# Batching three groups of VectorE instructions in a two-layer decoder trunk with an expert mixer

## The chip, the cores and the metric

One core of a Trainium2 chip runs the whole program. Its engines are TensorE (PE in the rows), which multiplies matrices, VectorE (DVE), ScalarE (ACT), GpSimd (POOL, which here only issues gathers) and SyncE (SP, which issues the other transfers). Each engine works through its own instructions in order and waits on semaphores for the others. The metric is the device time of one execution in microseconds (us), lower is better.

## The reference

The input is 512 tokens of width 1024. Each of two layers has a token mixer (retention and a gated recurrence), a cross-attention into 256 memory tokens, and a channel mixer that retrieves experts. The change is in the channel mixer:

```
s1 = q1 . sub_k1   s2 = q2 . sub_k2        # 8 heads, 128 keys each half
v1, i1 = top_k(s1, 16);  v2, i2 = top_k(s2, 16)
cand = v1[:, None] + v2[None, :]           # keep the best 16 of the pair sums
vals, ci = top_k(cand, 16)
idx = i1[ci // 16] * 128 + i2[ci % 16];    gates = softmax(vals)
act = gelu(peer_u[idx] . x)                # 16384 experts of width 1024
out = sum over 8 * 16 experts of gates * act * peer_v[idx]
```

## The kernel before

The channel mixer (`peer`) handles 384 of the 512 tokens densely: it multiplies all 128 blocks of 128 experts with all 384 tokens and weights the result by a gate table that is zero where an expert was not chosen. The last tile of 128 tokens is done by gathering expert rows, on POOL and DVE.

- **Keys.** For each of 16 half heads PE makes scores for the four token tiles, and DVE takes the best 16 with five instructions (`top16`, lines 834 to 839). One instruction for each half head and tile (line 853) turns the 16 indices into scaled key numbers. There are 64 of these in a layer.
- **U stage.** A loop over 128 blocks j of `peer_u`: 24 matmuls of 384 columns each on PE (three products for each of eight chunks, lines 216 to 218), then a gelu on ACT (`ag`, line 1030). Between the blocks the loop advances three generators at rates set by hand: `route` (line 878), `scatter` (line 979) and `rows_u` (line 776).
- **route(t)**, in the order of tiles 3, 0, 1, 2: the sums of the candidates, their best 16, and then for each head a look-up of the expert's number: a difference of 16 by 50 candidates (line 905) and a minimum of its absolute value (line 907), then the gates, and for tiles 0 to 2 three transposes on PE.
- **scatter**, for tiles 0 to 2 as each has been routed: for each group of four tokens DVE makes one-hot rows (`oab`, line 947, two buffers), ACT scales them by the gates (`ob`, line 953, two buffers; four instructions, or eight where the gate is in two halves), PE multiplies the two (`sm`, line 963 or 971) and ACT, in half of the groups with DVE, puts the result into `stage`. Every 16 tokens SP writes one stage of 1 MB to DRAM (`gates<-stage`, line 977).
- **rows_u**, after route(3): for each of 128 places a gather of one expert row for each of the 128 gathered tokens (`rows`, three buffers) and one product with the token's row on DVE (line 782).
- **V stage.** The loop over blocks runs from the last group of eight to the first. At the head of a group the gates of the group are read back from DRAM (`big<-gates` for the first one, `gg` later; line 807). For each block DVE multiplies activations by gates (`wv`, line 1066), `split` makes the two halves `ws` (ACT line 222, DVE line 223), and PE adds 24 matmuls of 384 columns into eight accumulators (`out`). `rows_v` advances beside it and adds one gathered row to `yrow` on DVE (line 800).
- **Weights.** For every block SP loads 512 KB (`w`, four buffers), ACT makes `wh` (line 200) and DVE makes `wl` (line 202), three buffers each; PE needs both.

Code is written in this order, but a list scheduler places the instructions of each engine by modelled times before the program is built, so the order on an engine may differ from that of the source, and a change of a few instructions can move many others.

Of the kernel before, what the change touches and what calls it, by code (L numbers as in the profile page):

```python
# [19 lines left out]
D = 1024  # L20
# [6 lines left out]
PH = 8  # L27
# [126 lines left out]
def trunk(ctx: ExitStack, tc: tile.TileContext, A, out, dbg=None):  # L154
# [84 lines left out]
    def C(n, t=cst, base=NTAB):  # L239
        o, w = CST[n]  # L240
        return t[:, o - base:o - base + w]
# [519 lines left out]
    def peer(l):  # L761
# [14 lines left out]
        def rows_u():  # L776
            for k in range(PH * K):
                r = gp.tile([128, D], F32, name="rows", bufs=3)
                nc.gpsimd.indirect_dma_start(out=r, out_offset=None, in_=A["peer_ur"].rearrange("l e d -> (l e) d"),  # L779
                                             in_offset=bass.IndirectOffsetOnAxis(ap=irow[:, 0, k:k + 1], axis=0))  # L780
                s = gp.tile([128, D], F32, name="prod", bufs=1)
                nc.vector.scalar_tensor_tensor(s, r, 1.0, hrow, op0=OP.mult, op1=OP.mult, accum_out=arow[:, k:k + 1])
                yield 1.3
                if k % 32 == 31:
                    ks = slice(k - 31, k + 1)
                    nc.scalar.activation(wrow[:, ks], arow[:, ks], AF.Gelu_apprx_tanh)
                    nc.vector.tensor_mul(wrow[:, ks], wrow[:, ks], grow[:, ks])
# [22 lines left out]
        with tpool(name=f"pr{l}", bufs=1) as rt, tpool(name=f"ph{l}", bufs=1) as hp, tpool(name=f"pps{l}", bufs=4, space=PS) as psum, \  # L810
# [30 lines left out]
            with tpool(name=f"pk{l}", bufs=1) as kp:  # L841
                def keys(hd, i, q, sk):
                    sc = psm.tile([128, TT, NK], F32, name="sm")
                    for t in range(TT):
                        nc.tensor.matmul(sc[:, t], lhsT=q[:, t * 128:(t + 1) * 128], rhs=sk, start=True, stop=True)
                    yield
                    s = kp.tile([128, TT, NK], F32, name="sc", bufs=3)
                    nc.scalar.copy(s, sc)
                    for t in range(TT):
                        wk = kp.tile([128, NK], F32, name="wk", bufs=2)  # L850
                        idx = kp.tile([128, K], U32, name="idx", bufs=2)
                        top16(val[i][t][:, hd], idx, s[:, t], wk)
                        nc.vector.scalar_tensor_tensor(idf[i][t][:, hd], idx, (NK if i == 0 else 1.0) / IDS,
                                                       C("first") if i == 0 else C("iota")[:, 0:K],
                                                       op0=OP.mult, op1=OP.add)

                for c in range(2 * PH):
                    hd, i = divmod(c, 2)
# [12 lines left out]
                        token_rows()  # L871
                drain()

            pp = es.enter_context(tpool(name=f"pu{l}", bufs=1))
            pe = pp.tile([128, TD, 2], F32, name="pe")
            pg = pp.tile([128, 3, TD], F32, name="pg")

            def route(t):

                big = gp.tile([128, NTB * GRP * TB], F32, name="big")  # L880
                cand, cid = (big[:, o:o + PH * NC_].rearrange("p (h c) -> p h c", h=PH) for o in (0, PH * NC_))
                ohs = [big[:, o:o + K * NC_].rearrange("p (k c) -> p k c", k=K)
                       for o in (2 * PH * NC_, 2 * PH * NC_ + K * NC_)]
                for dst, a1, a2 in ((cand, val[0][t], val[1][t]), (cid, idf[0][t], idf[1][t])):
                    off = 0
                    for a in range(8):
# [13 lines left out]
                cf = rt.tile([128, PH, K], F32, name="cf", bufs=2)  # L900
                nc.vector.tensor_copy(cf, ci)
                ee = rt.tile([128, PH, K], F32, name="ee", bufs=2)
                for hd in range(PH):
                    oh = ohs[hd % 2]
                    nc.vector.tensor_sub(oh, cid[:, hd, None, :].to_broadcast([128, K, NC_]),
                                         cf[:, hd, :, None].to_broadcast([128, K, NC_]))
                    nc.vector.tensor_reduce(ee[:, hd], oh, axis=AX.X, op=OP.min, apply_absolute_value=True)
                    yield 1.8
                ei = rt.tile([128, 3, PH * K], I32, name="ei", bufs=1)
                nc.vector.tensor_scalar(ei[:, 2], ee.rearrange("p h k -> p (h k)"), IDS, None, op0=OP.mult)  # L910
                nc.vector.tensor_scalar(ei[:, 1], ei[:, 2], NK - 1, None, op0=OP.bitwise_and)
# [133 lines left out]
        with tpool(name=f"pv{l}", bufs=1) as vp, tpool(name=f"vps{l}", bufs=1, space=PS) as psum:  # L1045
# [10 lines left out]
            for j in v_order():  # L1056
                g, i = divmod(j, GRP)
                if i == 0:
                    gg = gates.get(g) or gate_group(vp, f"gg{g % 2}", g)
                    if j < NK - GC * GRP:  # L1060
                        ar = vp.tile([128, GRP, TD], F32, name=f"ar{(g + 1) % 2}")
                        nc.sync.dma_start(ar, acts[g])
                kept = j - (NK - GC * GRP)
                act = ar[:, i] if kept < 0 else last[kept // 4][:, i % 4]
                wv = vp.tile([128, TD], F32, name="wv", bufs=2)
                nc.vector.tensor_mul(wv.rearrange("p (b t) -> p b t", b=NTB),
                                     act.rearrange("p (b t) -> p b t", b=NTB), gg[:, :, i, :])
                ws = vp.tile([128, 2, TD], F32R, name="ws", bufs=max(3, NCM))
                split(ws, wv)
                pend.append((weights("v", l, j, ahead=1 if j == GRP - 1 else 2), ws))  # L1070
                if not GRP - NCM <= j < GRP:
                    products(j, pend.pop())
                credit += VPACE
                while credit > 0:
                    credit -= next(todo, VPACE)
# [92 lines left out]
```

## Time and profile before

| | |
|---|---|
| median of three runs | 3853.55 us (3851.89 to 3855.34) |
| the profiled execution, its span | 3855.28 us, 3853.2 us |
| PE busy | 3801.3 us, 99% of the span |
| DVE busy | 2999.6 us, 78% |
| ACT busy | 1900.1 us, 49% |
| POOL busy | 734.3 us, 19% |
| DMA | 877.06 MB, mean 228 GB/s |

In time, one layer is the mixer and the attention (about 0 to 668 us in the first layer), keys and the U stage (about 694 to 1379 us) and the V stage (about 1381 to 1921 us); the second layer repeats it about 1917 us later. A row of the timeline gives the start, the duration, the engine and line, what is written from what, how many instructions are merged (x), and in brackets how long the engine was idle before and what ended it. Instructions of DVE and ACT overlap by a little, so the distance from one start to the next is shorter than a duration.

### The profile page before, as it was taken

What the parts mean: (1) busy time and instruction counts of PE and PEld (TensorE: products, weight loads), DVE (VectorE), ACT (ScalarE), POOL (GpSimd) and SP (SyncE); (2) the same over time, 40 slices, a digit from 0 to 9 for tenths busy, and PEclk for the clock granted to TensorE, in tenths of its full rate; (3) what the DMA queues carried; (4) which work ended last, traced back from release to release, by engine and by line L of the source; (5) the groups of instructions that cost most, each with busy time, mean ns of one, the idle gap of its engine ahead of it and who ended that gap; (6) DMA issues with size and microseconds to landing.
All of it is one profiled execution on the core that took longest, in us unless ns stands there. A gap on an engine that the chain in (4) does not pass through costs nothing.

```text
span 3853.2 us, 56299 instructions
## 1 busy us (share of the span) xinstructions
PE 3801.3 (99%) x20636; PEld 3535.2 (92%) x20636; DVE 2999.6 (78%) x5556; ACT 1900.1 (49%) x3531; POOL 734.3 (19%) x517
## 2 busy tenths in 40 slices
PE   8999999999999999999999999999999999999998
PEld 7888888899999999999978888878999999999998
DVE  7449665999989968777854596659999898687877
ACT  5336444336778843333343363543367788333333
POOL 0000000013233323333200000000232333233432
PEclk9999999999999999999999999999999999999999
DMA  4222342268999989999722223322689999899995
GB/s 150 82 87 95 104 134 69 83 208 317 309 319 348 335 325 338 345 346 346 269 82 77 93 94 104 131 67 88 232 308 312 319 350 315 332 348 342 345 346 213
DMA packets 313476, 877.06 MB, mean 228 GB/s; under 512 B 24945, under 2 KB 131569, under 8 KB 305265
## 3 DMA queue, kind: packets, MB, share of 16 engines
q1 hardware_dynamic: 239472, 605.01, 44.3%
q0 software_dynamic: 73728, 268.47, 19.8%
q8 instruction: 162, 2.65, 0.3%
q14 instruction: 114, 0.93, 0.1%
HBM read 776.13 MB, written 97.26 MB: 227 GB/s over the span
## 4 chain that ended last, share of the span: by engine, by line
PE 88%; DVE 8%; DMA 2%; issue 1%; ACT 1%; POOL 0%; SPq 0%; DVEq 0%; ACTq 0%; POOLq 0%
PE acc L216 18%; PE acc L218 18%; PE acc L217 18%; PE out L216 9%; PE out L217 9%; PE out L218 9%; PE sm L971 2%; DVE wl L202 2%; DMA rows<-peer_ur,irow 1%; PE sm L963 1%; DVE wk L837 1%; DVE idx L839 1%; DVE idx L836 1%; DVE val L838 1%; DVE val L835 1%
## 5 line engine op out<-in xcount | busy, mean ns | idle before, releaser
L200 ACT CAST wh<-w 128x1024 fp32r<-128x1024 f32 x768 | 802.0, 1049 | 1028.0 <-PE acc L217 662.7
L202 DVE TENSOR_TENSOR wl<-w,wh 128x1024 fp32r<-128x1024 f32 x768 | 935.1, 1218 | 338.9 <-ACT wh L200 315.5
L779 POOL DMA_INDIRECT rows<-peer_ur,irow x256 | 360.9, 1410 | 2354.9 <-DVE irow L927 1687.6
L216 PE MATMUL acc<-hf,wh 128*128 128x384 f32 (+1 forms) x2256 | 777.2, 344 | 7.3 <-DVE hf L223 6.1
L218 PE MATMUL acc<-hf,wl 128*128 128x384 f32 (+1 forms) x2256 | 775.9, 345 | 5.9 <-DVE wl L202 5.8
L217 PE MATMUL acc<-hf,wh 128*128 128x384 f32 (+1 forms) x2256 | 774.0, 343 | 0.0
L216 PE MATMUL out<-ws,wh 128*128 128x384 f32 x2048 | 687.6, 336 | 6.3 <-DVE ws L223 6.3
L217 PE MATMUL out<-ws,wh 128*128 128x384 f32 x2048 | 685.9, 335 | 0.0
L218 PE MATMUL out<-ws,wl 128*128 128x384 f32 x2048 | 575.8, 335 | 0.0
L216 PE MATMUL acc<-a,wh 128*128 128x512 f32 x1280 | 507.4, 397 | 15.9 <-ACT wh L200 10.5
L795 POOL DMA_INDIRECT rv<-peer_v,irow x256 | 373.0, 1457 | 716.6 <-DVE yrow L800 609.7
L217 PE MATMUL acc<-a,wh 128*128 128x512 f32 x1280 | 505.1, 395 | 0.0
L218 PE MATMUL acc<-a,wl 128*128 128x512 f32 x1280 | 503.8, 394 | 0.1
L216 PEld LDWEIGHTS acc<-hf,wh 128*128 128x128 f32 x2256 | 425.4, 189 | 17.9 <-DVE hf L223 8.7
L218 PEld LDWEIGHTS acc<-hf,wl 128*128 128x128 f32 x2256 | 425.1, 189 | 17.2 <-DVE wl L202 8.8
L217 PEld LDWEIGHTS acc<-hf,wh 128*128 128x128 f32 x2256 | 425.4, 189 | 7.8
L222 ACT CAST ws<-wv 128x384 fp32r<-128x384 f32 x256 | 131.1, 512 | 537.8 <-PE out L218 268.9
L216 PEld LDWEIGHTS out<-ws,wh 128*128 128x128 f32 x2048 | 385.8, 188 | 6.9 <-DVE ws L223 6.9
L217 PEld LDWEIGHTS out<-ws,wh 128*128 128x128 f32 x2048 | 385.7, 188 | 0.0
L953 ACT ACTIVATE ob<-oab,pg 128x128 fp32r<-128x128 f32 (+1 forms) x1152 | 357.2, 393 | 38.6 <-DVE oab L947 37.7
L218 PEld LDWEIGHTS out<-ws,wl 128*128 128x128 f32 x2048 | 375.9, 188 | 0.0
L800 DVE SCALAR_TENSOR_TENSOR yrow<-rv,wrow,yrow 128x1024 f32<-128x1024 f32 x254 | 324.5, 1278 | 50.9 <-DMA rv<-peer_v,irow 50.9
(291 smaller groups left out, 5186.5 us busy)
## 6 DMA issues: line engine op xcount, KB each, us to landing
w<-peer_u SPq DMA_DIRECT2D x256, 512.0 KB, 5.8
w<-peer_v SPq DMA_DIRECT2D x256, 512.0 KB, 6.3
gates<-stage SPq DMA_DIRECT2D x48, 1024.0 KB, 8.6
gg<-gates SPq DMA_DIRECT2D x30, 1536.0 KB, 9.0
acts<-ag SPq DMA_DIRECT2D x56, 768.0 KB, 6.2
ar<-acts SPq DMA_DIRECT2D x28, 1536.0 KB, 13.7
w<-w_f SPq DMA_DIRECT2D x80, 512.0 KB, 3.3
w<-w_t SPq DMA_DIRECT2D x32, 512.0 KB, 3.3
```

The lines of the kernel that those rows point to most:

```text
L200: nc.scalar.copy(wh, w)
L202: nc.vector.tensor_sub(wl, w, wh.bitcast(F32))
L216: nc.tensor.matmul(acc, lhsT=lh, rhs=rl, start=start, stop=False)
L217: nc.tensor.matmul(acc, lhsT=lh, rhs=rh, start=False, stop=False)
L218: nc.tensor.matmul(acc, lhsT=ll, rhs=rh, start=False, stop=stop)
L222: nc.scalar.copy(dst[:, 0], src)
L779: nc.gpsimd.indirect_dma_start(out=r, out_offset=None, in_=A["peer_ur"].rearrange("l e d -> (l e) d"), in_offset=bass.IndirectOffsetOnAxis ...
L795: nc.gpsimd.indirect_dma_start(out=r, out_offset=None, in_=pv, in_offset=bass.IndirectOffsetOnAxis(ap=irow[:, 1, k:k + 1], axis=0))
L800: nc.vector.scalar_tensor_tensor(yrow, r, wrow[:, k:k + 1], yrow, op0=OP.mult, op1=OP.add)
L835: nc.vector.max(v[:, 0:8], src)
L953: nc.scalar.activation(ob[:, i, k % 2], oh[:, 2 * i + 1].bitcast(F32), AF.Copy, scale=pg[:, k, t0 + i:t0 + i + 1])
L971: nc.tensor.matmul(g[:, i], lhsT=oh[:, 2 * i], rhs=ob[:, i, 0], start=True, stop=True)
```

## The change

1. The product of line 782 writes over the gathered row and no longer into a tile `prod` of its own.
2. Key numbers: `top16` writes its indices into the tile of the key numbers, and a new function `numbers(t)`, called at the head of route(t), converts all eight heads of a tile in one instruction of 128 columns for each half, in place.
3. Look-ups: two heads by one instruction (1600 columns), and one step of the generator (3.6) for two heads instead of two steps (1.8).
4. V stage: `wv` and the split `ws` are made for two blocks at once (768 columns); `ws` has two buffers of a pair instead of three of a block.

```diff
-                s = gp.tile([128, D], F32, name="prod", bufs=1)
-                nc.vector.scalar_tensor_tensor(s, r, 1.0, hrow, op0=OP.mult, op1=OP.mult, accum_out=arow[:, k:k + 1])
+                nc.vector.scalar_tensor_tensor(r, r, 1.0, hrow, op0=OP.mult, op1=OP.mult, accum_out=arow[:, k:k + 1])
...
-                        idx = kp.tile([128, K], U32, name="idx", bufs=2)
-                        top16(val[i][t][:, hd], idx, s[:, t], wk)
-                        nc.vector.scalar_tensor_tensor(idf[i][t][:, hd], idx, (NK if i == 0 else 1.0) / IDS,
-                                                       C("first") if i == 0 else C("iota")[:, 0:K],
-                                                       op0=OP.mult, op1=OP.add)
+                        top16(val[i][t][:, hd], idf[i][t][:, hd].bitcast(U32), s[:, t], wk)
...
+            def numbers(t):
+
+                for i, first in enumerate((C("first"), C("iota")[:, 0:K])):
+                    nc.vector.scalar_tensor_tensor(idf[i][t], idf[i][t].bitcast(U32), (NK if i == 0 else 1.0) / IDS,
+                                                   first[:, None, :].to_broadcast([128, PH, K]),
+                                                   op0=OP.mult, op1=OP.add)
+
...
-                for hd in range(PH):
-                    oh = ohs[hd % 2]
-                    nc.vector.tensor_sub(oh, cid[:, hd, None, :].to_broadcast([128, K, NC_]),
-                                         cf[:, hd, :, None].to_broadcast([128, K, NC_]))
-                    nc.vector.tensor_reduce(ee[:, hd], oh, axis=AX.X, op=OP.min, apply_absolute_value=True)
-                    yield 1.8
+                for hd in range(0, PH, 2):
+                    nc.vector.tensor_sub(oh, cid[:, hd:hd + 2, None, :].to_broadcast([128, 2, K, NC_]),
+                                         cf[:, hd:hd + 2, :, None].to_broadcast([128, 2, K, NC_]))
+                    nc.vector.tensor_reduce(ee[:, hd:hd + 2], oh, axis=AX.X, op=OP.min, apply_absolute_value=True)
+                    yield 3.6
...
-                wv = vp.tile([128, TD], F32, name="wv", bufs=2)
-                nc.vector.tensor_mul(wv.rearrange("p (b t) -> p b t", b=NTB),
-                                     act.rearrange("p (b t) -> p b t", b=NTB), gg[:, :, i, :])
-                ws = vp.tile([128, 2, TD], F32R, name="ws", bufs=max(3, NCM))
-                split(ws, wv)
-                pend.append((weights("v", l, j, ahead=1 if j == GRP - 1 else 2), ws))
+                if i % 2 == 0:
+                    act = ar[:, i:i + 2] if kept < 0 else last[kept // 4][:, i % 4:i % 4 + 2]
+                    wv = vp.tile([128, 2, TD], F32, name="wv", bufs=2)
+                    nc.vector.tensor_mul(wv.rearrange("p j (b t) -> p j b t", b=NTB),
+                                         act.rearrange("p j (b t) -> p j b t", b=NTB),
+                                         gg[:, :, i:i + 2, :].rearrange("p b j t -> p j b t"))
+                    ws = vp.tile([128, 2, 2, TD], F32R, name="ws", bufs=2)
+                    split(ws, wv)
+                pend.append((weights("v", l, j, ahead=1 if j == GRP - 1 else 2), ws[:, :, i % 2]))
```

The first place is the passage from U to V, on ACT. Before, from the scaling of the last group of four tokens to the first halves `ws` of the V stage, it read:

```order
L953 ACTIVATE ob<-oab,pg 128x128 x4
L972 COPY stage<-sm 128x128x4
L200 CAST wh<-w 128x1024
L1030 ACTIVATE ag<-acc 128x384
L972 COPY stage<-sm 128x128x4
L200 CAST wh<-w 128x1024
L1030 ACTIVATE ag<-acc 128x384
L200 CAST wh<-w 128x1024
L1030 ACTIVATE ag<-acc 128x384
L200 CAST wh<-w 128x1024
L1030 ACTIVATE ag<-acc 128x384
L222 CAST ws<-wv 128x384 x3
```

After the last copy of a stage stand three more gelus, that is three blocks of U. Now, from the gelu of the last block on, the same engine reads:

```order
L1031 ACTIVATE ag<-acc 128x384
L954 ACTIVATE ob<-oab,pg 128x128 x4
L973 COPY stage<-sm 128x128x4
L954 ACTIVATE ob<-oab,pg 128x128 x8
L973 COPY stage<-sm 128x128x4
L954 ACTIVATE ob<-oab,pg 128x128 x8
L967 COPY stage<-sm 128x128x2 x2
L954 ACTIVATE ob<-oab,pg 128x128 x4
L967 COPY stage<-sm 128x128x2 x2
L954 ACTIVATE ob<-oab,pg 128x128 x4
L973 COPY stage<-sm 128x128x4 x2
L222 CAST ws<-wv 128x768 x2
```

Five scalings and all copies of six groups have moved behind the last gelu of U.

The second place is the same passage on PE (`hf` is the normalised input, `out` the V stage's accumulators; each row of `sm` with x8 is two groups). Before, U's last matmuls are followed at once by V's:

```order
L218 MATMUL acc<-hf_5170,wl 128x384
L216 MATMUL acc<-hf_5171,wh 128x384
L217 MATMUL acc<-hf_5171,wh 128x384
L218 MATMUL acc<-hf_5171,wl 128x384
L216 MATMUL out_13172<-ws,wh 128x384
L217 MATMUL out_13172<-ws,wh 128x384
```

Now it reads:

```order
L216 MATMUL acc<-hf_5171,wh 128x384
L217 MATMUL acc<-hf_5171,wh 128x384
L218 MATMUL acc<-hf_5171,wl 128x384
L972 MATMUL sm<-ob,oab 128x128 x8
L964 MATMUL sm<-ob,oab 128x256 x8
L972 MATMUL sm<-ob,oab 128x128 x8
L216 MATMUL out_12923<-ws,wh 128x384
L217 MATMUL out_12923<-ws,wh 128x384
```

Six groups of four tokens stand behind U's last matmul, where the last group stood 71 matmuls ahead of U's end.

The third place is the look-ups of tile 0 on DVE. Before:

```order
L782 SCALAR_TENSOR_TENSOR prod,arow<-rows,hrow 128x1024
L905 TENSOR_TENSOR big<-big,cf 128x800 x2
L202 TENSOR_TENSOR wl<-w,wh 128x1024
L920 RECIPROCAL gsum<-gsum 128x8
L907 TENSOR_REDUCE ee<-big 128x16
L782 SCALAR_TENSOR_TENSOR prod,arow<-rows,hrow 128x1024
L907 TENSOR_REDUCE ee<-big 128x16
L202 TENSOR_TENSOR wl<-w,wh 128x1024
```

Now:

```order
L908 TENSOR_REDUCE ee<-big 128x32
L921 RECIPROCAL gsum<-gsum 128x8
L781 SCALAR_TENSOR_TENSOR rows,arow<-rows,hrow 128x1024
L202 TENSOR_TENSOR wl<-w,wh 128x1024
L781 SCALAR_TENSOR_TENSOR rows,arow<-rows,hrow 128x1024
L906 TENSOR_TENSOR big<-big,cf 128x1600
L922 TENSOR_TENSOR ex<-ex,gsum 128x128
L781 SCALAR_TENSOR_TENSOR rows,arow<-rows,hrow 128x1024
L202 TENSOR_TENSOR wl<-w,wh 128x1024
```

The products of gathered rows stand closer together. When tile 2, the last to be routed, has been routed, DVE has made 63 of these products in the order before, and 86 now; its transposes stand on PE after 73.2 blocks of U before, and after 80.1 now. The last of the 128 products comes in block 124 before, and in block 115 now. Both layers have the same order in this.

## Rows read from the trace of the kernel before

**Rows 1.** Groups of PE's waits: us in total, times, longest.
```profile
PE out L216 <- DVE ws L223: 6.3, 2, 3.6
```
**Rows 2.** Stretches (keys and early U, both layers; mid V): PE, PEld, DVE, ACT, POOL, clock.
```profile
694.00:870.00 176.00, 172.29 (x945) 159.60 (x943) 168.53 (x834) 66.48 (x94) 18.11 (x13) 0.99 0.47 156
2611.00:2790.00 179.00, 175.57 (x961) 162.50 (x960) 172.60 (x839) 67.46 (x95) 19.20 (x14) 0.99 0.49 160
...
1600.00:1880.00 280.00, 280.00 (x1618) 280.00 (x1617) 225.72 (x271) 99.28 (x136) 111.55 (x70) 1.00 0.91 346
```
**Rows 3.** Stretches just after PE had waited: the same columns.
```profile
855.50:859.00 3.50, 3.50 (x13) 3.50 (x12) 3.50 (x9) 3.08 (x5) 1.13 (x2) 0.51 0.80 294
...
1381.20:1384.60 3.40, 3.11 (x10) 3.11 (x11) 2.76 (x6) 0.51 (x1) 0.00 (x0) 0.50 1.03 422
...
3299.50:3306.30 6.80, 5.62 (x18) 5.63 (x19) 3.64 (x7) 0.58 (x2) 0.00 (x0) 0.50 1.04 431
```
**Rows 4.** Timeline from U to V, first layer, PE and DVE.
```profile
1365.43 1.05 PE L971 MATMUL sm<-ob,oab 128*128 128x128 f32 x8
...
1378.46 0.34 PE L218 MATMUL acc<-hf,wl 128*128 128x384 f32 x1
1378.72 1.03 DVE L1066 TENSOR_TENSOR wv<-ag,big 128x384 f32<-128x384 f32 x2 [1.91 <-DMA big<-gates]
1379.74 1.23 DVE L202 TENSOR_TENSOR wl<-w,wh 128x1024 fp32r<-128x1024 f32 x1
1380.88 1.02 DVE L223 TENSOR_TENSOR ws<-wv,ws 128x384 fp32r<-128x384 f32 x2
...
1381.49 0.69 PE L216 MATMUL out<-ws,wh 128*128 128x384 f32 x1 [2.69 <-DVE ws L223]
```
**Rows 5.** The chain that ended last, same place: start, us, what.
```profile
1367.22 5.11 DMA gates<-stage
1372.39 6.31 DMA big<-gates
```
**Rows 6.** Timeline from U to V, second layer, PE.
```profile
3283.74 1.05 PE L971 MATMUL sm<-ob,oab 128*128 128x128 f32 x8
...
3300.68 0.69 PE L216 MATMUL out<-ws,wh 128*128 128x384 f32 x1 [3.56 <-DVE ws L223]
```
**Rows 7.** Timeline of ACT late in U, first layer.
```profile
1351.33 2.44 ACT L953 ACTIVATE ob<-oab,pg 128x128 fp32r<-128x128 f32 x8
1353.68 0.56 ACT L972 COPY stage<-sm 128x512 f32<-128x512 f32 x1
...
1357.56 0.48 ACT L1030 ACTIVATE ag<-acc 128x384 f32<-128x384 f32 x1
1357.94 0.64 ACT L966 COPY stage<-sm 128x256 f32<-128x256 f32 x2
1358.77 1.28 ACT L953 ACTIVATE ob<-oab,pg 128x128 f32<-128x128 f32 x4 [0.19 <-DVE oab L947]
```
**Rows 8.** Groups on DVE: busy us, mean ns of one, idle before.
```profile
L202 DVE TENSOR_TENSOR wl<-w,wh 128x1024 fp32r<-128x1024 f32 x768 | 935.1, 1218 | 338.9 <-ACT wh L200 315.5 <-PE sm L496 13.1 <-PE sm L507 8.5
...
L905 DVE TENSOR_TENSOR big<-big,cf 128x800 f32<-128x800 f32 x64 | 61.4, 979 | 0.1
...
L853 DVE SCALAR_TENSOR_TENSOR idf<-idx,cst 128x16 f32<-128x16 uint32 x128 | 20.0, 158 | 0.0
```
**Rows 9.** Timeline of DVE in the first look-ups.
```profile
817.04 1.88 DVE L905 TENSOR_TENSOR big<-big,cf 128x800 f32<-128x800 f32 x2
818.84 0.97 DVE L907 TENSOR_REDUCE ee<-big 128x16 f32<-128x800 f32 x1
```
**Rows 10.** DMA issues: us from issue to landing; and a DVE wait: us, times, longest.
```profile
rows<-peer_ur,irow POOLq DMA_INDIRECT x256, 7.4
...
DVE prod L782 <- DMA rows<-peer_ur,irow: 27.9, 22, 3.7
```

More of the change, by code (lines that the diff above doesn't have):

```diff
@@ L881, in route @@
                 cand, cid = (big[:, o:o + PH * NC_].rearrange("p (h c) -> p h c", h=PH) for o in (0, PH * NC_))
-                ohs = [big[:, o:o + K * NC_].rearrange("p (k c) -> p k c", k=K)
-                       for o in (2 * PH * NC_, 2 * PH * NC_ + K * NC_)]
+                oh = big[:, 2 * PH * NC_:2 * PH * NC_ + 2 * K * NC_].rearrange("p (h k c) -> p h k c", h=2, k=K)
+                numbers(t)
                 for dst, a1, a2 in ((cand, val[0][t], val[1][t]), (cid, idf[0][t], idf[1][t])):
@@ L1063, in peer @@
                 kept = j - (NK - GC * GRP)
-                act = ar[:, i] if kept < 0 else last[kept // 4][:, i % 4]
-                wv = vp.tile([128, TD], F32, name="wv", bufs=2)
-                nc.vector.tensor_mul(wv.rearrange("p (b t) -> p b t", b=NTB),
-                                     act.rearrange("p (b t) -> p b t", b=NTB), gg[:, :, i, :])
-                ws = vp.tile([128, 2, TD], F32R, name="ws", bufs=max(3, NCM))
-                split(ws, wv)
-                pend.append((weights("v", l, j, ahead=1 if j == GRP - 1 else 2), ws))
+                if i % 2 == 0:
[7 more added lines that the diff above has]
+                pend.append((weights("v", l, j, ahead=1 if j == GRP - 1 else 2), ws[:, :, i % 2]))
                 if not GRP - NCM <= j < GRP:
```

## The prediction

> **What bounds the kernel now.** I first read the busy time by stretches. In the middle of V, PE is busy 280.00 of 280 us while DVE works 225.72 us [rows 2], so a shorter `wv` or `ws` there buys nothing. 1618 matmuls in 280 us are one in 0.173 us, a block of 24 in 4.15 us. So the second reading was where PE waits at all. Two places bear on the change. From keys into early U, DVE works nearly without a pause (168.53 of 176 us and 172.60 of 179 us), and PE, which needs its `wl`, is idle for 176 - 172.29 = 3.7 us in the first layer and 179 - 175.57 = 3.4 us in the second [rows 2]. From U to V, PE waits once in each layer for the halves `ws`, together 6.3 us [rows 1], 2.69 us and 3.56 us [rows 4, 6].
>
> The third reading was the chain behind that last wait. The last scatter group's matmuls start at 1365.43 us. ACT copies them, and SP writes the stage (issued at 1367.22 us, landed after 5.11 us), then reads the gates back (issued at 1372.39 us, landed after 6.31 us), because the first group of V needs the gates of all tokens [rows 5]. Then DVE makes two `wv`, a `wl` and the first `ws`, and V's first matmul starts at 1381.49 us [rows 4]: 16.06 us from the group's matmuls to V. In the second layer it is 3300.68 - 3283.74 = 16.94 us [rows 6]. Most of this is hidden because U still has work: its last matmul starts at 1378.46 us, 13.0 us after the group [rows 4]. The kernel has a cover of about three blocks, and it is almost used up.
>
> After such a wait PE's granted clock reads 0.50, the 1.2 GHz level: for 3.4 us in the first layer and 6.8 us in the second after U's end, and 0.51 for 3.5 us after a wait in early U [rows 3]. Half speed costs half of such a stretch.
>
> **What the change saves.** 800 columns take 979 ns and 1024 take 1218 ns [rows 8], 1.07 ns a column. Two look-up differences and the next start are 818.84 - 817.04 = 1.80 us apart [rows 9], so back to back one takes 0.90 us. 800 columns of that are 0.85 us, and an instruction saved is worth 0.05 us; by whole durations it would be 0.979 - 0.854 = 0.125 us. DVE runs back to back in this stage, so I take the lower end.
>
> - Look-ups: 64 instructions become 32 in a layer, 1.6 us (4.0 us by durations).
> - Key numbers: 64 of 16 columns become 8 of 128. By durations, 64 x 0.158 [rows 8] = 10.1 us become 8 x (0.158 + 112 x 0.00107) = 2.2 us, saving 7.9 us. Back to back, with 0.075 us off each, 5.3 us become 1.6 us, saving 3.7 us.
> - Products in place: the same 1024 columns, so no time. What goes is the order between successive products that shared one `prod` tile.
> - V stage: 256 DVE instructions become 128 in a layer, at 0.05 to 0.125 us each, and 64 fewer on ACT. PE covers all of it. Were PE not the bound there, the same amount could at most come back, 6 to 16 us a layer.
>
> So about 5 us of DVE work (up to 12) leaves the stretch in which DVE is late. What PE can get back there is its idle time, 3.7 and 3.4 us, and what the half clock cost, about 1.7 us in the first layer and by estimate the same in the second: 10.5 us in all. Half of the saved work stands behind PE's last wait of the stretch, so I take **5 us** for both layers, with 0 and 10.5 us as ends.
>
> The Trainium skill (VectorE: DVE Perf Modes, "The TRN2 errata") gives a Vector instruction (N + 151) / 0.96 ns, so each one removed would save 157 ns. The single durations here agree (991 ns for 800 columns, 979 measured), but the spacing of 0.90 us [rows 9] contradicts it as a cost of an instruction in a row. By the page the look-ups and key numbers would save some 14 us a layer; by the spacing it is 5.
>
> **What it moves.** The order on the engines has changed far beyond the edits. Products of gathered rows stand closer together, 86 instead of 63 when tile 2 has been routed. DVE is full there, so the extra 23, at the 1.2 us of an instruction of this width [rows 8], push routing back by 27 us, some seven blocks of U. Tile 2's scatter starts that much later and ends behind U. Six of its groups now stand on PE and ACT after U's last block, which nothing covers. PE runs in order, so it can't take them earlier.
>
> After U's end ACT must do the last gelu, then for the groups in turn scalings of four, eight, eight, four and four, and the copies between them, before PE can multiply the last group. With `ob` and `oab` in two buffers they can't be made ahead. From durations: 0.48 + 3 x 1.28 + 2 x 2.44 + 2 x 0.56 + 2 x 0.64 = 11.6 us, of which overlaps take about 0.1 us at each of ten joints (a gelu of 0.48 us is followed after 0.38 us) [rows 7]. ACT may have to wait for an `oab` in between; I take **11 us**. From there the chain of before follows, 16.06 and 16.94 us. Its end is different work of the same length: two `wv` and one `ws` of 768 columns, about 0.05 + 0.82 us each, 2.6 us, where two `wv`, a `wl` and a `ws` took 1381.49 - 1378.72 = 2.77 us [rows 4]. On SP the gates' read waits for the last write, and behind it stand the reads of the next gates and activations and the loads of V's weights; in SP's order seven of those loads stand ahead of it, so the first blocks' weights aren't late.
>
> V therefore starts 27.1 us after U's last matmul in the first layer and 27.9 us in the second. PE is not idle for all of that: the six groups' matmuls (1.05 us for four tokens [rows 4], less for the groups in halves, together about 5 us) were done inside U before. Idle are 22.1 and 22.9 us, against 2.69 and 3.56 us: **19.4 us more in each layer, 38.8 us**. I expect the longer half-clock stretch, 6.8 us, after both: **1.7 us**.
>
> The Trainium skill (DMA: Bandwidth & Descriptors, "Rules for kernel authors") says to issue a transfer early and to wait late, so that its fixed cost overlaps. This speaks against the change: the write and the read are now issued with no computation left beside them, and their 11.4 us [rows 5] are paid.
>
> **The sum.** 38.8 + 1.7 - 5 = 35.5 us on the profiled execution's 3855.3 us gives 3890.8 us. That execution is 1.7 us above the median of 3853.55 us, so the forecast is 3890 us, 0.9% slower.
>
> Bounds: the write and read could be faster with fewer transfers beside them, by an estimated 1.5 us, and ACT's sequence shorter by 2 us where a scaling is already under way; with all 10.5 us gained in early U this gives 3890 - 7 - 5.5 - 1.7 = 3876 us. On the other side, no gain in early U (5 us), waits for `oab` of 3 us a layer and reads that are slowed by those queued behind them by the same give about 3907 us.
>
> **The rivals.**
> - *Faster.* The tail is hidden and DVE's saving counts: 10.5 us less at most, some 3843 us. It needs the last group's matmuls to stand at least 13 us ahead of U's end, the point from which V's wait is no longer than before. For it speak DVE's saturation and PE's waits for `wl`; against it, PE's order. By the Trainium skill's 157 ns (the section above) it would have 28 us of DVE work to win with, but PE has no such idle time there [rows 2].
> - *No difference.* Tail and gain cancel, 3846 to 3861 us: only if the tail were a third of what I worked out, with V's wait growing by 5 us a layer and all of early U's idle time gone.
> - *Much slower.* The denser products wait for their gathers. A gather lands after 7.4 us and three buffers are in turn, so with a product of 1.2 us one every 2.9 us is possible; the order wants 72 in blocks 16 to 73, where before it had 59, and 57 blocks of 4.15 us and some scatter are about 250 us, so one in about 3.5 us. Before, DVE waited 27.9 us in 22 times [rows 10]. If the spacing is uneven enough that half of these 72 wait another 0.5 us, that is 18 us a layer on an engine which PE is waiting for: some 3926 us.
>
> **Chances.** The forecast, a tail of 15 to 25 us a layer, 0.82; much slower 0.09; no difference 0.04; faster 0.05. The range of 3873 to 3909 us leaves out most of the rivals and some of the forecast's own edges, about 2 in 10. A change of 0.2%, 7.7 us, is about what a measurement of this kernel can tell from none; slower by more than that has 0.91.
>
> **What would show it.** Right: in both layers a gap on PE of 20 to 25 us before V's first matmul, broken by scatter's matmuls, with the last write of the gates issued about 13 us after U's last matmul, and half clock after it. Early U's PE waits for `wl` shrink below 3 us a layer. V's spacing stays 0.173 us. Wrong: scatter's matmuls run before U's end, or V starts within 10 us of it; or DVE's waits for gathered rows grow to several times 27.9 us.

## The result, and the profile after

The changed kernel takes 3898.38 us (median; 3895.28 to 3900.18) against 3853.45 us for the kernel before in the same comparison: 1.0115 times as long, with a 95% interval of 1.0099 to 1.013. The profiled execution took 3900.18 us, its span is 3898.4 us, 45.2 us more than before. The forecast was 3890 us, with a range of 3873 to 3909 us.

Where the 45.2 us lie shows when the positions of four matmuls in PE's timeline are compared: the first and last of U, the first and last of V.

| starts, us | U, first to last | U's last to V's first | V, first to last |
|---|---|---|---|
| before, layer 1 | 608.17 | 3.03 | 535.79 |
| before, layer 2 | 609.29 | 3.91 | 536.94 |
| after, layer 1 | 606.93 | 28.21 | 535.83 |
| after, layer 2 | 605.45 | 28.38 | 536.91 |

The passage from U to V grew by 25.18 and 24.47 us, U got shorter by 1.24 and 3.84 us, V is the same to 0.04 us. Together that is 44.6 us; the rest, 0.6 us, lies ahead of the first U.

The passage of the first layer, timeline of PE in the kernel after (start, duration, engine, line, what is written from what; in brackets the idle time before and what ended it), answers to [rows 4]:

```profile
1377.83 0.34 PE L218 MATMUL acc<-hf,wl 128*128 128x384 f32 x1
1378.00 1.05 PE L972 MATMUL sm<-ob,oab 128*128 128x128 f32 x8
1379.80 1.36 PE L972 MATMUL sm<-ob,oab 128*128 128x128 f32 x8 [0.75 <-ACT ob L954]
1381.74 0.39 PE L964 MATMUL sm<-ob,oab 128*128 128x256 f32 x1 [0.58 <-ACT ob L954]
...
1387.13 3.93 PE L972 MATMUL sm<-ob,oab 128*128 128x128 f32 x16 [0.25 <-ACT ob L954]
1406.04 0.69 PE L216 MATMUL out<-ws,wh 128*128 128x384 f32 x1 [14.98 <-DVE ws L223]
```

Six groups of scatter (40 matmuls, `sm`) stand between U's last matmul and V's first. Up to the last two of them PE is stopped again and again by ACT, whose own timeline in the same place answers to [rows 7]:

```profile
1378.98 0.48 ACT L1031 ACTIVATE ag<-acc 128x384 f32<-128x384 f32 x1
1379.36 1.27 ACT L954 ACTIVATE ob<-oab,pg 128x128 f32<-128x128 f32 x4
...
1380.99 2.45 ACT L954 ACTIVATE ob<-oab,pg 128x128 fp32r<-128x128 f32 x8
...
1383.80 2.45 ACT L954 ACTIVATE ob<-oab,pg 128x128 fp32r<-128x128 f32 x8
...
1388.53 1.28 ACT L954 ACTIVATE ob<-oab,pg 128x128 f32<-128x128 f32 x4
```

The last group's matmuls, alone in the timeline of PE in the first layer, answer to the first row of [rows 4]:

```profile
1389.00 2.06 PE L972 MATMUL sm<-ob,oab 128*128 128x128 f32 x8
```

They start 11.17 us after U's last matmul, and the same in the second layer. From there it is 17.04 us to V, and 17.21 us in the second layer. The chain that ended last goes through the write of the stage and the reading of the gates (start, duration), as in [rows 5]:

```profile
1391.71 5.09 DMA gates<-stage
1396.85 6.30 DMA big<-gates
```

and DVE, idle for 14.07 us until the gates have landed, makes the products of the first two pairs of blocks and the first halves `ws`:

```profile
1403.17 1.83 DVE L1068 TENSOR_TENSOR wv<-ag,big 128x768 f32<-128x768 f32 x2 [14.07 <-DMA big<-gates]
1405.03 1.83 DVE L223 TENSOR_TENSOR ws<-wv,ws 128x768 fp32r<-128x768 f32 x2
```

The stretches (PE, PEld, DVE, ACT, POOL busy with counts, granted clock, DMA share, GB/s): keys and early U in both layers, mid V, the passage of the first layer and its second part, and the first microseconds of V in both layers, for [rows 2, 3]:

```profile
694.00:870.00 176.00, 172.32 (x948) 160.32 (x947) 166.65 (x771) 66.89 (x94) 21.41 (x15) 0.99 0.47 158
2635.60:2814.60 179.00, 176.36 (x972) 164.55 (x971) 171.82 (x776) 68.49 (x96) 22.85 (x16) 0.99 0.49 166
...
1625.00:1905.00 280.00, 280.00 (x1617) 280.00 (x1616) 226.12 (x206) 94.97 (x101) 91.60 (x67) 1.00 0.92 342
...
1378.20:1406.00 27.80, 9.75 (x40) 7.13 (x38) 10.75 (x16) 14.28 (x40) 3.75 (x4) 0.63 0.67 230
...
1385.00:1406.00 21.00, 5.60 (x19) 4.36 (x19) 5.50 (x10) 7.48 (x21) 3.75 (x4) 0.51 0.81 278
...
1406.00:1409.40 3.40, 3.36 (x11) 3.36 (x12) 3.26 (x4) 0.00 (x0) 0.00 (x0) 0.54 0.98 410
...
3345.80:3351.20 5.40, 5.30 (x17) 5.30 (x18) 3.32 (x5) 0.00 (x0) 0.94 (x1) 0.50 1.01 425
```

V runs at 1617 matmuls in 280 us as before. PE starts V at the 1.2 GHz level, for 3.1 us and 5.4 us; before it was 3.1 and 5.6 us of V. But now the clock has fallen well ahead of V, while scatter's matmuls were still running with waits between them: from 1385 to 1406 us it is 0.51. The last group's eight matmuls took 2.06 us at that level, where a group took 1.05 us before [rows 4]. In keys and early U of the first layer, DVE works 1.9 us less and PE has gained 0.03 us; in the second layer both figures are 0.8 us.

PE's waits over the whole kernel (us, times, longest) and DVE's for gathered rows, for [rows 1, 10]:

```profile
PE out L216 <- DVE ws L223: 30.1, 2, 15.2
...
PE acc L218 <- DVE wl L202: 8.8, 10, 2.5
PE sm L964 <- ACT ob L954: 7.0, 13, 1.8
...
PE sm L972 <- ACT ob L954: 2.0, 4, 0.7
...
DVE rows L781 <- DMA rows<-peer_ur,irow: 38.6, 33, 4.2
```

Before, the waits for `wl` were 5.8 us in 6 times, and those for `ob` 0.4 us. Of the 9.0 us for `ob` now, about 6 us lie in the two passages. The longest wait for `wl` within U, first before and then now (DVE, DVE, PE):

```profile
851.55 1.23 DVE L782 SCALAR_TENSOR_TENSOR prod<-rows,hrow 128x1024 f32<-128x1024 f32 x1 [3.71 <-DMA rows<-peer_ur,irow]
...
853.01 1.21 DVE L202 TENSOR_TENSOR wl<-w,wh 128x1024 fp32r<-128x1024 f32 x1
854.27 0.45 PE L218 MATMUL acc<-hf,wl 128*128 128x384 f32 x1 [2.30 <-DVE wl L202]
```

```profile
852.68 1.23 DVE L781 SCALAR_TENSOR_TENSOR rows<-rows,hrow 128x1024 f32<-128x1024 f32 x1 [3.96 <-DMA rows<-peer_ur,irow]
...
854.13 1.21 DVE L202 TENSOR_TENSOR wl<-w,wh 128x1024 fp32r<-128x1024 f32 x1
855.40 0.44 PE L218 MATMUL acc<-hf,wl 128*128 128x384 f32 x1 [2.54 <-DVE wl L202]
```

Both times DVE had stood still for a gathered row just ahead of the `wl`, for longer than PE then waits.

DVE's instructions themselves cost what their columns say (busy, mean ns, idle before), for [rows 8]:

```profile
L906 DVE TENSOR_TENSOR big<-big,cf 128x1600 f32<-128x1600 f32 x32 | 58.2, 1818 | 0.2
...
L872 DVE SCALAR_TENSOR_TENSOR idf<-idf,cst 128x128 f32<-128x128 uint32 x16 | 4.4, 274 | 0.0
```

The timeline of DVE shows a look-up difference and the instruction behind it, for [rows 9]:

```profile
812.54 1.82 DVE L906 TENSOR_TENSOR big<-big,cf 128x1600 f32<-128x1600 f32 x1
814.28 1.22 DVE L202 TENSOR_TENSOR wl<-w,wh 128x1024 fp32r<-128x1024 f32 x1
```

From its start to the next, a difference for two heads takes 814.28 - 812.54 = 1.74 us, where two for one head each took 1.80 us [rows 9]: the pair saves 0.06 us. Counted like this over both layers, up to its end or to the next start where that comes first, the look-ups take 3.7 us less of DVE's time and the key numbers 6.8 us less, 10.5 us in all.

### The profile page after: what moved, and what is told of

Its sections match the earlier page's. It is cut to its first block, busy times and chain, and to the rows that moved or that the text cites. A ratio compares the mean times of both kernels' runs of the same rounds, so it can differ in the third digit from the quotient of the medians.

```text
span 3898.4 us, 55483 instructions
## 1 busy us (share of the span) xinstructions
PE 3811.8 (98%) x20636; PEld 3541.2 (91%) x20636; DVE 2976.2 (76%) x5124; ACT 1886.1 (48%) x3403; POOL 726.0 (19%) x517
## 4 chain that ended last, share of the span: by engine, by line
PE 87%; DVE 5%; DMA 3%; issue 2%; ACT 1%; POOL 1%; SPq 0%; DVEq 0%; POOLq 0%; ACTq 0%
PE acc L216 18%; PE acc L218 18%; PE acc L217 18%; PE out L216 9%; PE out L217 9%; PE out L218 9%; PE sm L972 2%; DMA rows<-peer_ur,irow 2%; DVE wl L202 1%; PE sm L964 1%; POOL rows L779 1%; PE sm L216 1%; PE sm L217 1%; PE sm L218 1%; DVE wk L836 0%
## 5 line engine op out<-in xcount | busy, mean ns | idle before, releaser
L216 PE MATMUL out<-ws,wh 128*128 128x384 f32 x2048 | 687.5, 336 | 30.1 <-DVE ws L223 30.1
L794 POOL DMA_INDIRECT rv<-peer_v,irow x256 | 362.3, 1415 | 853.8 <-DVE yrow L799 613.0
L781 DVE SCALAR_TENSOR_TENSOR rows<-rows,hrow 128x1024 f32<-128x1024 f32 x256 | 311.3, 1219 | 39.0 <-DMA rows<-peer_ur,irow 38.6
```

Of the source, the lines that this page charges most:

```text
L216: nc.tensor.matmul(acc, lhsT=lh, rhs=rl, start=start, stop=False)
L781: nc.vector.scalar_tensor_tensor(r, r, 1.0, hrow, op0=OP.mult, op1=OP.mult, accum_out=arow[:, k:k + 1])
L794: nc.gpsimd.indirect_dma_start(out=r, out_offset=None, in_=pv, in_offset=bass.IndirectOffsetOnAxis(ap=irow[:, 1, k:k + 1], axis=0))
```

## The experiments

**Theory.** The loss is an order, and not what any single instruction costs. The single product tile `prod` made each product of a gathered row wait in the scheduler's model for the one before. Without that chain the products crowd into the first half of U, routing comes later, and the last scatter groups fall behind U. The batches as such are neutral or better. **Rivals:** writing over the gathered row costs time itself, since a row's buffer is held by it; or the batches cost it. The table gives the same distances as above, layer 1 / layer 2, and DVE's waits for gathered rows; these come from one profiled execution of each kernel, the medians from all.

| kernel | median us, ratio to before (95%) | U, first to last | U to V | gather waits us, times |
|---|---|---|---|---|
| before | | 608.2 / 609.3 | 3.0 / 3.9 | 27.9, 22 |
| after | 3898.4, 1.0115 (1.0099 to 1.013) | 606.9 / 605.5 | 28.2 / 28.4 | 38.6, 33 |
| 1 own product tile | 3852.8, 0.9994 (0.9985 to 1.0003) | 610.1 / 607.7 | 3.4 / 3.4 | 32.3, 26 |
| 2 in place alone | 3913.4, 1.0151 (1.0135 to 1.0166) | 610.2 / 616.1 | 30.8 / 30.1 | 52.4, 41 |
| 3 two row buffers | 3968.3, 1.0294 (1.028 to 1.0308) | 664.9 / 660.6 | 9.6 / 8.1 | 225.4, 115 |
| 4 four row buffers | 3912.3, 1.0147 (1.0132 to 1.0163) | 600.9 / 600.5 | 40.4 / 39.2 | 15.4, 17 |
| 5 paced later | 3875.1, 1.0056 (1.0042 to 1.007) | 614.4 / 618.5 | 4.2 / 7.1 | 47.8, 42 |
| 6 own tile, two buffers | 3896.3, 1.0112 (1.0096 to 1.0127) | 610.5 / 608.4 | 25.5 / 25.6 | 41.2, 45 |
| 7 own tile, four row buffers | 3842.8, 0.9975 (0.9966 to 0.9984) | 603.2 / 604.3 | 3.0 / 3.7 | 15.9, 11 |
| 8 the same, paced | 3838.9, 0.9968 (0.9957 to 0.9979) | 602.6 / 602.5 | 3.0 / 3.0 | 7.5, 7 |
| 9 as 8, no batches | 3847.9, 0.9986 (0.9977 to 0.9995) | 606.6 / 605.5 | 3.3 / 3.3 | 10.1, 9 |
| 10 as 8, V pairs too | 3840.5, 0.9971 (0.9962 to 0.9981) | 602.2 / 601.8 | 3.4 / 3.4 | 5.5, 6 |
| 11 V pairs alone | 3854.6, 1.0006 (0.9997 to 1.0015) | 608.5 / 609.8 | 4.7 / 4.3 | 28.7, 27 |

The order itself can be counted in the traces. When tile 2 has been routed, DVE has made 63 products in the kernel before and 86 after; with one product tile it is 64 in run 1 and 66 in run 7, with two product tiles 85 in run 6, and in place 85 in run 2, 100 with four row buffers (run 4) and 53 with two (run 3).

**1. Own product tile, all batches kept.** In the kernel after:

```diff
-                nc.vector.scalar_tensor_tensor(r, r, 1.0, hrow, op0=OP.mult, op1=OP.mult, accum_out=arow[:, k:k + 1])
+                s = gp.tile([128, D], F32, name="prod", bufs=1)
+                nc.vector.scalar_tensor_tensor(s, r, 1.0, hrow, op0=OP.mult, op1=OP.mult, accum_out=arow[:, k:k + 1])
```

> All of the change but the product in place: the product of a gathered row goes to a tile of its own again. Theory (the product in place lets the products of gathered rows run ahead in the order, routing and scatter come late, and six scatter groups stand uncovered between U and V): here the last group stands 95 matmuls, 16.4 us, ahead of U's end, so V starts with a wait of under 1 us in each layer and nearly no half clock; the time falls below the kernel before, to 3838 to 3848 us. Rival (the batching of look-ups, key numbers or V pairs makes V start late): the wait at V's start stays at 15 to 20 us a layer and the time at 3885 to 3900 us.

One product tile takes the tail away: 3852.8 us. That the rival falls is clear; that the kernel would beat the one before was wrong. V's wait stays, though the gates are there in time, as the timeline of the passage shows (DVE, ACT, PE):

```profile
1378.97 1.82 DVE L1069 TENSOR_TENSOR wv<-ag,big 128x768 f32<-128x768 f32 x2
...
1381.85 0.48 ACT L1032 ACTIVATE ag<-acc 128x384 f32<-128x384 f32 x1
1381.98 1.23 DVE L202 TENSOR_TENSOR wl<-w,wh 128x1024 fp32r<-128x1024 f32 x1 [1.19 <-ACT wh L200]
1382.23 1.55 ACT L222 CAST ws<-wv 128x768 fp32r<-128x768 f32 x2
1383.12 1.82 DVE L223 TENSOR_TENSOR ws<-wv,ws 128x768 fp32r<-128x768 f32 x2
...
1384.13 0.65 PE L216 MATMUL out<-ws,wh 128*128 128x384 f32 x1 [3.09 <-DVE ws L223]
```

`wv` was made 5 us ahead, but the halves `ws` stand behind U's last gelu on ACT and behind a `wl` on DVE. And U did not get shorter, with DVE waiting more for gathered rows (32.3 us) than before.

**2. In place alone**, the diff above the other way round on the kernel before, without the batches.

> The kernel before with the product in place and nothing else. Theory: seven scatter groups stand behind U's last block, V starts some 28 us after U's end, the time is 3898 to 3910 us, as slow as the whole change or slower. Rival (batching at fault): 3850 to 3857 us.

3913.4 us, worse than the whole change and 3.4 us above the range that the theory gave: the tail comes without any batch, longer (30.8 and 30.1 us) than the 28 us expected. PE's waits in it, with those for `wl` at more than twice the 8.8 us of the kernel after:

```profile
PE out L216 <- DVE ws L223: 32.0, 2, 16.3
PE acc L218 <- DVE wl L202: 20.4, 18, 3.9
```

So the batches give back some 15 us of what the product's edit costs.

**3 and 4. Two, and four, buffers for the gathered rows**, in the kernel after; the diff is that of the first, the second has a 4 in the same place:

```diff
-                r = gp.tile([128, D], F32, name="rows", bufs=3)
+                r = gp.tile([128, D], F32, name="rows", bufs=2)
```

> The whole change, with two buffers for gathered rows instead of three, so that fewer products fit between the blocks: 53 of them by the time tile 2 is routed, against 86, and the last scatter group 179 matmuls (31 us) ahead of U's end. Theory: V starts without a wait, 3838 to 3852 us, unless DVE's waits for gathers grow beyond 30 us a layer. Rival (writing over the gathered row is itself slow, or the V pairs are): still 3880 us or more.

> The whole change, with four buffers for gathered rows: 100 products by the time tile 2 is routed, ten scatter groups behind U's end instead of six. Theory: four more groups at 1.8 to 3.1 us of ACT each, less their PE time, are about 7 us more idle PE a layer, so 3908 to 3918 us. Rival (the loss comes from DVE waiting for gathers): a fourth buffer takes those waits away and the time falls below 3890 us.

With two buffers the time expected was missed, by the exception that the expectation named: products are spread, the tail shrinks to 8 or 9 us, but DVE waits 225.4 us for rows, and PE for what DVE makes late, in U itself:

```profile
PE acc L218 <- DVE wl L202: 25.9, 23, 2.6
PE sm L972 <- DVE stage L968: 24.8, 10, 6.8
...
DVE rows L781 <- DMA rows<-peer_ur,irow: 225.4, 115, 6.7
```

With four buffers the gathers hardly hold DVE up (15.4 us), yet the time is 3912.3 us: the products crowd still more, ten groups stand behind U, and V waits 40 us. The time is in the range expected. The two runs show the order and the gathers as two separate costs.

**5. The whole change, the scatter's pace raised.**

```diff
-GPACE = 1.0
+GPACE = 1.3
```

> The whole change, products in place and all batches kept; only the planner's figure for the pace of the gathers (GPACE) is raised from 1.0 to 1.3. By the order of the instructions the last scatter group then stands 71 matmuls ahead of U's end in layer 1 and 48 in layer 2 (none, with six groups behind it, in the kernel after), while the token-row products stay as close together as after (tile 2 is routed 89 products in, after 86, before 63). My theory: the 27 us tail behind each U is the loss, and it hangs on the order alone, so it goes: PE's wait at V's start 3 us in layer 1 and at most 9 us in layer 2, early-U waits as after (about 10 us a layer), 3855 to 3870 us. Rival (the denser gathers or the batches themselves cost the time): 3885 us or more.

GPACE is the rate of `scatter` in the loop over U's blocks, and not that of the gathers, as this expectation and a later one call it. The tail goes, with products in place and all batches. That is the theory's main point. But it is only half of the loss: 3875.1 us is still 21.7 us above the kernel before, and 5 us above the range expected, because U grew to 614.4 and 618.5 us. Some 5 us a layer of that are scatter's matmuls, which are in U again. The rest is PE idle, 8.9 and 12.1 us within U against 6.3 and 5.5 us in the kernel after, most of it waiting for `wl`, and DVE waits 47.8 us for rows. The second layer's longest case, in DVE's timeline, ahead of a PE wait of 3.6 us:

```profile
2960.94 1.23 DVE L781 SCALAR_TENSOR_TENSOR rows<-rows,hrow 128x1024 f32<-128x1024 f32 x1 [2.17 <-DMA rows<-peer_ur,irow]
...
2965.40 1.22 DVE L781 SCALAR_TENSOR_TENSOR rows<-rows,hrow 128x1024 f32<-128x1024 f32 x1 [1.44 <-DMA rows<-peer_ur,irow]
...
2967.68 1.22 DVE L202 TENSOR_TENSOR wl<-w,wh 128x1024 fp32r<-128x1024 f32 x1
```

**6. Own product tile with two buffers**, all batches kept:

```diff
-                nc.vector.scalar_tensor_tensor(r, r, 1.0, hrow, op0=OP.mult, op1=OP.mult, accum_out=arow[:, k:k + 1])
+                s = gp.tile([128, D], mybir.dt.bfloat16, name="prod", bufs=2)
+                nc.vector.scalar_tensor_tensor(s, r, 1.0, hrow, op0=OP.mult, op1=OP.mult, accum_out=arow[:, k:k + 1])
```

> The whole change, but the product of a token row goes into a tile of its own again, as before, now in bf16 and with two buffers, so that two successive products no longer share one tile. Only the accumulated sum is used, so the narrower product tile changes nothing in the result. By the order of the instructions the scatter groups stand behind U's end again (about five groups late). My theory: what the old single product tile did was to order one product behind the one before it in the planner's eyes, and it is that spacing that was lost with the in-place form; so this one is slow like the kernel after, 3885 to 3905 us, with PE waiting 20 to 27 us in two waits at V's starts. Rival (writing over the gathered row, which holds its buffer longer, is what costs): 3850 to 3860 us.

As slow as the kernel after, and with the same two waits, which are longer than the 20 to 27 us expected:

```profile
PE out L216 <- DVE ws L223: 31.1, 2, 15.8
```

Beside run 1, only the second buffer and the narrower type differ, and run 7 has the narrower type with one buffer and no tail. So what counts is that two successive products no longer share one tile; that the product is written elsewhere changes nothing here. A product in place with the order kept was not tried.

**7 and 8. One product tile, four row buffers**, key numbers and look-ups batched, V's blocks single; the second also with the pace of 1.3. Against the kernel before, besides those two batches:

```diff
-            sq = part if c == 0 else pool.tile([128, n], F32, name="sq", bufs=SQB)
+            sq = part if c == 0 else pool.tile([128, n], F32, name="sq", bufs=1 if name == "sm" else SQB)
...
-                r = gp.tile([128, D], F32, name="rows", bufs=3)
+                r = gp.tile([128, D], F32, name="rows", bufs=4)
...
-                s = gp.tile([128, D], F32, name="prod", bufs=1)
+                s = gp.tile([128, D], mybir.dt.bfloat16, name="prod", bufs=1)
```

> One product tile with one buffer as before (in bf16, which frees room), key numbers and look-ups batched as in the change, V's blocks one by one as before, four buffers instead of three for the gathered rows, and one buffer fewer for the squares in one place to pay for it. By the order of the instructions the last scatter group stands 72 matmuls ahead of U's end (71 before) and the products are spread as before (tile 2 is routed 66 products in). My theory: with the tail as before and one more row in flight DVE's waits for gathered rows fall from 28 us to 15 us or less as with four buffers in the run ahead, early-U waits of PE fall from 7 to about 5 us a layer, and the kernel ends at 3842 to 3852 us, a little under before. Rival (the early-U waits of PE have another cause than the gathers, or the second square buffer was needed): 3853 us or more.

> The kernel of the run ahead (own product tile in bf16 with one buffer, four row buffers, key numbers and look-ups batched) with the gathers' pace figure raised from 1.0 to 1.3. By the order of the instructions the last scatter group stands 117 matmuls ahead of U's end instead of 72. My theory: PE's wait at V's start is held at about 3 us by the first split that stands behind the last of U's work on DVE, and no longer by the scatter, so the earlier scatter saves nothing beyond the run ahead: within 4 us of it. Rival (the last scatter still sets V's start there): 5 to 8 us faster than the run ahead.

Both beat the kernel before: 10.6 us less, and 14.5 us less (medians, against 3853.39 us), both as expected; the 3.9 us between the two are not clear of the noise, since their intervals overlap. In the second one U is shorter by 5.5 and 6.8 us. PE is idle 3.0 and 3.3 us less in it, and by estimate another 1.7 us a layer is the stretch at half clock in early U, which doesn't occur: the granted clock is 1.00 from 694 to 870 us and from 2611 to 2790 us. What is left of PE's early waits is

```profile
PE out L216 <- DVE ws L223: 5.4, 2, 2.7
...
PE acc L218 <- DVE wl L202: 1.2, 2, 0.8
...
DVE prod L782 <- DMA rows<-peer_ur,irow: 7.5, 7, 1.5
```

A product into bf16 takes 1216 ns, one into 32 bits 1217 ns in run 1; the narrow type only makes room.

**9. The same without the batches** (the kernel before with the three edits of run 8 and its pace):

> The kernel before with none of the change, but with what the fastest run so far had beside it: the product tile in bf16 with one buffer, four buffers for the gathered rows, one buffer fewer for the squares in one place, and the pace figure 1.3. What it lacks against that run is only the batched key numbers and look-ups. By the order of the instructions its last scatter group stands 72 matmuls ahead of U's end (117 there). My theory: nearly all of that run's 14 us came from DVE's waits for gathered rows (28 us in the kernel before, 7.5 us there), so this one ends at 3838 to 3848 us with at most 15 us of such waits. Rival (the batches give the gain, by leaving DVE free earlier): 3850 us or more.

3847.9 us: at the upper end of what the theory allowed, and "nearly all from the gathers" was wrong. Four buffers, the narrow tile and the pace alone shorten U by 1.6 and 3.8 us; with the batched key numbers and look-ups U is another 3.9 and 3.0 us shorter. The size is rough: the intervals of the two ratios just touch, and the order moved as well (117 matmuls behind the last scatter group in run 8, 72 here). Its waits for `wl` are over four times those of run 8:

```profile
PE acc L218 <- DVE wl L202: 5.6, 5, 2.2
```

**10 and 11. V's pairs**, added to run 8, and alone on the kernel before:

> The fastest run so far (own product tile in bf16 with one buffer, four row buffers, pace 1.3, key numbers and look-ups batched) with V's products and splits for two blocks added, so that of the change only the in-place product is missing. The last scatter group stands 117 matmuls ahead of U's end in both. My theory: DVE is not what V waits for except at its start, so the pairs save nothing on the path, and the first split, now over two blocks, ends about 0.9 us later in each layer (1.82 us for the pair in place of 1.02 us): 3837 to 3844 us. Rival (DVE's shorter instructions in V let the row sums and splits come earlier): 3836 us or less; other rival (the pair doubles what PE waits for within V too): 3848 us or more.

> The kernel before with one part of the change alone: V's products and splits for two blocks. The order of the scatter and of the products in U is that of before. My theory: neutral, since the two V starts become at most 1 us longer each and nothing else moves, 3850 to 3858 us. Rival (V pairs cost on their own): 3862 us or more.

Neutral both times, as expected: the ratios can't be told from those of the kernels without the pairs. The passage is 0.4 to 1.7 us longer in each layer, probably as the first split is of two blocks, and V itself gains nothing from them (536.0 and 535.9 us in run 11; PE was busy all the time in mid V before [rows 2]).

## Why the prediction was right, and where not

- **The tail.** Predicted: V starts 27.1 and 27.9 us after U's last matmul, 5 us of it being matmuls that were in U before. Measured 28.2 and 28.4 us. The last group's matmuls start 11.2 us after U's last (11 were taken), and the write and the read take 5.09 and 6.30 us as before. PE is idle for less of the passage than the 22.1 us predicted, 18.0 us in the first layer, because the scatter's matmuls keep it busy for 9.75 us there and not for 5, in part at half clock. The Trainium skill's rule quoted in the prediction (DMA: Bandwidth & Descriptors, "Rules for kernel authors"), to issue a transfer early and wait for it late, is borne out: before, the reading of the gates ended 0.2 us after U's last matmul started (1372.39 + 6.31 against 1378.46 us), and now all 11.4 us stand behind U. That the tail comes from the order and not from the batches is shown by runs 1 and 2, 5 and 6.
- **What made the order.** The prediction named the order between products that shared one tile as what goes, but priced it only through DVE's fullness. Run 6 confirms it (85 products by the time that tile 2 is routed, against 64 in run 1); run 4 shows that with more rows in flight the crowding gets worse (100).
- **The half clock.** Predicted: 1.7 us more behind V's start. Measured: none there, V's length is the same to 0.04 us. The lower clock came earlier, inside the passage, where the last group's matmuls took 2.06 us in place of 1.05 us: about 1.0 us a layer by that difference.
- **Early U, the step that failed.** The prediction turned DVE's saving into 5 us of PE's time. With that, and with about 5 us of matmuls moved out of each layer's U, U should have been 15 us shorter in both layers together. It is 5.1 us shorter, so what stayed in it got 4.9 us longer. The saving on DVE was there: 10.5 us in both layers, 5.2 us a layer where the prediction's lower figure was 5.3 us. It did not reach PE, which is idle for 11.8 us within U in both layers together, where it was 7.5 us.
- **What PE waited for in U.** 3.0 us more for `wl`, and 2.6 us more for `ob` further into U (1.2 and 1.8 us, against 0.4 us), while a wait of 1.2 us for `wh` is gone, which the prediction had read as one for `wl`. The sign that the waits for `wl` would shrink below 3 us a layer failed: they are 5.1 and 3.7 us. The longest of them shows one reason. The prediction took `wl` to be late because DVE has too much work, but here it is late, before and after, because DVE stood waiting for a gathered row (3.71 and 3.96 us). An instruction saved ahead of such a wait only lets DVE arrive at it earlier. The other waits were not followed back one by one. The rival "much slower" named this mechanism, denser products that wait for their gathers; it was there, but small: DVE waits 10.7 us more for rows. Where these waits are mostly gone, U is shorter with the batches by 6.9 us in both layers (run 8 against run 9), by estimate 1.7 us of that through a stretch at half clock that run 9 has in its first layer and run 8 has not. What each of the two batches gives by itself was not separated.
- **The price of an instruction.** The single durations fit the Trainium skill's formula (VectorE: DVE Perf Modes, "The TRN2 errata"): (1600 + 151) / 0.96 = 1824 ns, measured 1818. As a saving the Trainium skill's 157 ns for each instruction would be some 28 us for the two batches in both layers; counted from start to start it was 10.5 us, as the spacing in [rows 9] had said.

The sum by its terms: passages 49.7 - 10 for the matmuls that moved = 39.7 us where 38.8 was predicted (by estimate some 2 us of it the lower clock), half clock behind V's start 0 instead of 1.7, early U +4.9 instead of -5, elsewhere 0.6: 45.2 us instead of 35.5. The small errors of the other terms nearly cancel, and the 10 us of early U are nearly the whole difference; the range held because its upper end allowed for no gain there and for waits in the tail that did not come. (The forecast's last step is rounded up: 3890.8 - 1.7 is 3889.1 us.)

## What to carry to other kernels

Under a scheduler that orders by modelled times, a scratch tile with one buffer is also an ordering rule: removing it moved 40 matmuls of each layer behind the end of a stage here, so read the new order of the engines before counting the instructions saved, above all whether the producer of a stage's last input still ends ahead of the stage. A saving on an engine may count only once that engine doesn't wait for a transfer itself: here, with the order of before, the batches were worth nothing (run 1), and some 7 us once a fourth buffer had taken most of the waits for gathered rows away (run 8 against run 9). And edits of which one loses alone (run 2) and the others do not (run 1) should be timed apart, since together they show only their sum.

## What the runs showed of the hardware

- Gathered rows: a gather lands in 7.6 us (7.4 before), and the number of buffers decides what DVE sees of it: 225.4 us of waits with two, 38.6 us with three and 15.4 us with four, at the same number of gathers.
- A pause of 15 us cost V no more of the 1.2 GHz level than one of 3 us: 3.1 and 5.4 us of V after the long pauses, 3.1 and 5.6 us after the short ones [rows 3]. Short pauses differed: in the second layer of runs 8 and 9 the granted clock stays at 1.00 after V's start, though PE had stood for some 3 us. Behind U in the kernel after, the clock fell already during matmuls with waits between them (0.51 from 1385 to 1406 us).
- Instructions of DVE in a row start closer together than they last. Medians from one start to the next, over the traces before and after: 0.469 us for 384 columns, 0.869 for 768, 0.902 for 800, 1.136 for 1024 and 1.736 us for 1600. That is 1.04 ns a column and 0.07 us for the instruction, so joining two into one of the double width saves about 0.07 us.
